# A decoder layer with routed experts on one core: row stores on ACT's queue, the first pair's overflow expert by expert, the last pair by halves of the columns

## The chip, the cores and the metric

One core of a Trainium2 chip. The metric is the time of one execution on the device in microseconds (us); several runs give a median. Times inside an execution are read from one profiled execution and count from the start of its span.

## The reference, cut to what matters

Batch 1, 512 tokens, width 1024, all float32. One layer: attention and a gating MLP side by side, then a mixture of 32 experts in 4 groups of 8.

```python
hn = rmsnorm(h, attn_norm_g); proj = hn @ w_in            # 1024 -> 2560
h = h + concat(rmsnorm(stick_breaking(q, k, v)), rmsnorm(gating(u, vg))) @ w_out
hn = rmsnorm(h, ffn_norm_g)
# one group by argmax, its two best experts; combine = p_group * renormalised p_expert
for g in range(4):                                        # the reference runs all experts
    a = silu(hn @ w_gate[g]) * (hn @ w_up[g])             # 1024 -> 512, per expert
    out = out + (a * combine[:, g]) @ w_down[g]           # 512 -> 1024
return rmsnorm(h + out, final_norm_g)
```

Each expert has 6 MB of weights (2 MB each for gate, up and down); together they are 192 MB that have to be read once. A token goes to two experts, so an expert has some 32 tokens of its own.

## The kernel before, in words

**Stages.** Up to some 215 us the kernel does the projection, attention, gating and the output product. From there on each block of 128 tokens (`c` = 0 to 3) gets its output product (lines 116 to 118, from `u_step`), is added to `h` (DVE, line 621), squared (ACT, 725), transposed (TensorE, 748), sent through the router (`route`, DVE, 757 to 797) and, normalised, stored to DRAM: `with_gain` (POOL, line 737; the last half on DVE) writes `h` times the gain to a tile `xn`, of which there are two, and `store_xn` (739 to 742) scales it on ACT and stores it to `xn_d`. The tile of block 0 is used again for block 2. Behind the router, the list of tokens by expert is built, and POOL gathers rows of `xn_d` by an indirect DMA: 64 slots for each of the two experts of a pair, 128 rows of 4 KB.

**The experts.** 16 pairs (loop from line 1150). For each: `gu(e)` multiplies the gathered rows with the gate and up weights (line 974, two halves of TensorE's columns at once), ACT copies the result (980), `act(e)` transposes and applies the gate (992, 984, 986), `combine` adds the pair before into `h` (TensorE 1028, DVE 1034), `down(p)` makes the down products of both experts (1001), `results(p)` splits them into a high and a low part (ACT 1019, DVE 1020). Up to 32 rows that do not fit into the 64 slots are kept apart; `gate_up_over` and `down_over` work on them under a branch, taken if the expert has such rows (`if_over`: TensorE, ACT and DVE each load a count and jump).

**The order of the loads.** Each weight tile of 1 MB has a slot in a ring; 19 slots exist when the experts begin. SP issues all loads in one list (`order`, line 574): for each pair eight of gate and up, then four of down. `load_next(n)` issues the next `n`, each as soon as the work that read the slot's last content is done. In the loop, `load_next(8)` stands behind both experts' gate and up products and their overflow branch, and `load_next(4)` behind the down products and theirs. Ahead of the loop, SP also issues the four stores of `xn_d` between its loads, and a small store `mark_d` that holds it until the first gather has landed. Each DMA of SP also waits until the DMA eight places ahead of it in its row of semaphores is done.

**The tail.** After the last pair: the one-hot of the overflow rows (1191, 1011), `down` with both halves of the columns in one go (1001), the overflow's own result (1197, 1198), `results`, then eight units (block, half of the columns): three products each (1225, 1028), a sum into `h` (1034) and a sum of squares (ACT, 1204); `scale_3` makes the scale (DVE 1208, POOL 1209), `finish` multiplies with the final gain (DVE 1218, in two cases ACT 1215 and POOL 1216) and stores 256 KB (1219).

Of the kernel before, what the change touches and what calls it, by code (L numbers as in the profile page):

```python
# [19 lines left out]
P = 128  # L20
T = 512
NCH = 4
D = 1024
KD = 8
NH = 8
E = 32
F = 512
# [44 lines left out]
def layer_kernel(ctx, tc, xr, xT, gT, w_inT, w_inR, sgg, wsT, bsp, sbg, sog, w_out, ffp, ffg, wr, br,  # L72
# [501 lines left out]
    order = []  # L574
    for p in range(E // 2):
        order += [(2 * p + r, i, j) for r in range(2) for j in range(2) for i in range(2)]
        order += [(2 * p + r, 2, j) for j in range(2) for r in range(2)]
    slots = []

    def half_slot(pool, tag="b"):  # L580
# [2 lines left out]
    def load_next(n=1):  # L583
        for _ in range(min(n, len(order))):
            e, i, j = order.pop(0)
            slots.append(slots.pop(0))
            t_ = slots[-1](f"r{e}_{i}_{j}")
            dma(t_, (w_gate, w_up, w_down)[i][e][:, j * 2048:(j + 1) * 2048])
            for m in range(2):
                W[e, i, 2 * j + m] = t_[:, m * 1024:(m + 1) * 1024]  # L590
# [356 lines left out]
    XS, GU, SG, HT, YS, OHT = {}, {}, {}, {}, {}, {}  # L947

    def bank(name, *shape):
        return psm.tile([P, *shape], F32, tag="m", name=name)  # L950
# [41 lines left out]
            nc.tensor.transpose(ft[:, j], SG[e][:, j], identf)  # L992
        HT[e] = gated(e, ft, SLOTS, "g")

    def down(p, n_last=False):
        YS[p] = [bank(f"y{p}_{n}", 512) for n in range(2)]
        for j, n in ([(0, 0), (0, 1), (1, 0), (1, 1), (2, 0), (3, 0), (2, 1), (3, 1)] if n_last else
                     [(j, n) for j in range(4) for n in range(2)]):
            for r, rs_ in halves:
                e = 2 * p + r  # L1000
                nc.tensor.matmul(YS[p][n][rs_], HT[e][:, j], W[e, 2, j][:, n * 512:(n + 1) * 512],  # L1001
                                 start=j == 0, stop=j == 3, skip_group_check=True)

    def places(p):
# [9 lines left out]
    def results(p):  # L1014

        yh, yl = (mo.tile([P, D], F32R, tag=t_, name=f"{t_}{p}") for t_ in ("yh", "yl"))
        for n in range(2):
# [4 lines left out]
        YS[p] = (yh, yl)  # L1022

    def add_rows(ps, p, u, first, last):

        c, n = divmod(u, 2)
        for i, y in enumerate(YS[p]):
# [90 lines left out]
    def gate_up_over(p):  # L1118

        for r in range(2):  # L1120
            so[2 * p + r] = xgo[:, r * 512:(r + 1) * 512].rearrange("s (j p) -> s j p", j=4)
        with if_over(66 + p):
            for e in (2 * p, 2 * p + 1):
                with if_over(34 + e):
                    ps = psg.tile([P, F], F32, tag="gu", name=f"go{e}")
                    for kk in range(4):
                        for q, rs_ in enumerate(quads):
                            k, i = 2 * kk + q // 2, q % 2
                            nc.tensor.matmul(ps[rs_], xso[:, k], W[e, i, kk][:, k % 2 * 512:(k % 2 + 1) * 512],
                                             start=kk == 0, stop=kk == 3, skip_group_check=True)  # L1130
                    nc.scalar.activation(so[e], ps.rearrange("s (p j) -> s j p", j=4), AF.Copy,
                                         scale=tabo[:, 2 + e:3 + e])

    def down_over(p):
        with if_over(66 + p):  # L1135
            for e in (2 * p, 2 * p + 1):
                with if_over(34 + e):
                    ft = bank(f"fo{e}", 4, SLOTS)
                    for j in range(4):
                        nc.tensor.matmul(ft[:, j], so[e][:, j], fold, start=j == 0, stop=j == 3,  # L1140
                                         skip_group_check=True)
                    ht = gated(e, ft, OVER, "o")
                    for jj in range(2):
                        for q, rs_ in enumerate(quads):
                            j, n = 2 * jj + q % 2, q // 2
                            nc.tensor.matmul(yo[rs_], ht[:, j], W[e, 2, j][:, n * 512:(n + 1) * 512], start=False,
                                             stop=False, skip_group_check=True)


    for p in range(NP):  # L1150
        a, b = 2 * p, 2 * p + 1
        gu(a)
        if p == 0:
            prep(xso, xgo, "o")
            clear(True)
            pst = bank("pst", 2, NP)
            for i in range(8):
                for r, rs_ in halves:
                    nc.tensor.matmul(pst[rs_], ohf[:, i], cf[:, i, :, r::2], start=i == 0, stop=i == 7,
                                     skip_group_check=True)  # L1160
# [32 lines left out]
    down(p, True)  # L1193
    yo2 = mo.tile([P, 2, 512], F32R, tag="xs", name="yo2")
    YO = [yo2[:, n] for n in range(2)]
    for n, rs_ in halves:
        nc.scalar.activation(YO[n][:SLOTS], yo[rs_], AF.Copy, scale=tabo[rs_, 1:2])
        nc.vector.scalar_tensor_tensor(YO[n][SLOTS:], yo[rs_], tabo[rs_, 1:2], YO[n][:SLOTS].bitcast(F32),
                                       op0=OP.mult, op1=OP.subtract)
    results(p)  # L1200
    ms3 = mo.tile([P, NCH, 2], F32, name="ms3")
    rs3 = mo.tile([P, NCH], F32, name="rs3")
    def squares(c, n):
        nc.scalar.activation(sq, h[:, c, n * 512:(n + 1) * 512], AF.Square, scale=1.0 / 32.0,  # L1204
                             accum_out=ms3[:, c, n:n + 1])
# [5 lines left out]
    def finish(c, n, shared=False):  # L1211
        cs = slice(n * 512, (n + 1) * 512)
        to, src, sc = fin[c][:, cs], h[:, c, cs], rs3[:, c:c + 1]
        if shared:
            nc.scalar.activation(to, src, AF.Copy, scale=sc)  # L1215
            nc.gpsimd.tensor_tensor(to, to, finB[:, cs], op=OP.mult)
        else:
            nc.vector.scalar_tensor_tensor(to, src, sc, finB[:, cs], op0=OP.mult, op1=OP.mult)  # L1218
        dma(out[c * P:(c + 1) * P, cs], to)

    sq = mo.tile([P, 512], F32, tag="sg", bufs=2, name="sq")

    def unit(c, n):
        ps = bank(f"cl{c}_{n}", 512)
        nc.tensor.matmul(ps, oho[:, c * P:(c + 1) * P], YO[n], start=True, stop=False, skip_group_check=True)
        add_rows(ps, p, 2 * c + n, False, True)
        into_h(ps, 2 * c + n)
        squares(c, n)
# [80 lines left out]
    with tc.If(n_over > OVER):  # L1309
# [20 lines left out]
            squares(c, 1)  # L1330
            scale_3(c)
        for c in range(NCH):
            for n in range(2):
                finish(c, n)
    begin.close()


# [52 lines left out]
```

## Time and profile before

| | us |
|---|---|
| median of 3 runs | 768.15 (763.91 to 768.45) |
| the profiled execution | 767.29 |
| its span | 765.5 |
| TensorE busy | 707.2 (92%) |
| DVE busy | 307.5 (40%) |
| ACT busy | 215.1 (28%) |
| POOL busy | 95.6 (12%) |
| moved by DMA | 231.59 MB, mean 303 GB/s |

The busy time of an engine is the union of its instructions; an engine that is busy need not be the one that the others wait for. Rows of a timeline give start, duration, engine, line, operation, result and operands, a count where equal rows are merged, and in square brackets the idle time ahead and what ended it. `PEq`, `SPq` and the like are an engine's sequencer.

### The profile page before, as it was taken

How to read it: one execution, taken by the hardware profiler on the slowest of the kernel's cores; microseconds unless marked ns; L12 is line 12 of the kernel's file. 1: busy time of each engine (PE TensorE's matmuls, PEld its weight loads, DVE VectorE, ACT ScalarE, POOL GpSimd, SP SyncE). 2: the span in 40 equal slices, each digit the busy share in tenths (PEclk: the TensorE clock that was granted, in tenths of full speed). 3: DMA queues.
4: the chain of work that ended last, by engine and by line, in shares of the span. 5: the costliest groups of instructions: out<-in, count | busy, mean ns of one | idle time of the engine just before them, and what ended most of it. 6: DMA issues, size and time to landing. Idle time of an engine off the chain costs nothing. (4 is left out here: it accounts for less than half of the span.)

```text
span 765.5 us, 9186 instructions
## 1 busy us (share of the span) xinstructions
PE 707.2 (92%) x3426; PEld 400.1 (52%) x3426; DVE 307.5 (40%) x538; ACT 215.1 (28%) x328; POOL 95.6 (12%) x88
## 2 busy tenths in 40 slices
PE   9999999999999699999999988999999999898991
PEld 7776666778787544443443434344344444244350
DVE  5556848455764811322431404033043133043065
ACT  6565755655433301111111111111111111111123
POOL 1322212115243310000000000000000000000003
PEclk9999979899999599999999999999999999999996
DMA  8711000217359339999999999999999999999933
GB/s 294 311 45 67 25 30 28 83 52 304 125 218 417 132 131 371 418 420 418 419 420 420 417 422 418 421 419 421 418 419 417 421 419 419 419 419 420 417 132 115
DMA packets 41435, 231.59 MB, mean 303 GB/s; under 512 B 6290, under 2 KB 7954, under 8 KB 16786
## 3 DMA queue, kind: packets, MB, share of 16 engines
q1 hardware_dynamic: 39010, 226.43, 72.8%
q0 software_dynamic: 2352, 4.20, 1.5%
q8 instruction: 44, 0.72, 0.4%
q14 instruction: 29, 0.24, 0.1%
HBM read 230.74 MB, written 4.19 MB: 307 GB/s over the span
## 5 line engine op out<-in xcount | busy, mean ns | idle before, releaser
L974 PE MATMUL gu<-r,xs 128*64 128x512 f32 x1024 | 230.5, 596 | 12.8 <-DMA r<-w_up 8.1
L974 PEld LDWEIGHTS gu<-r,xs 128*64 128x64 f32 x1024 | 84.4, 137 | 158.2 <-issue 134.1
L1001 PE MATMUL y<-r,hg 128*64 128x512 f32 x512 | 114.1, 595 | 3.3 <-ACTq L1135 2.9
L986 DVE TENSOR_TENSOR hg<-ft,gg 128x256 f32<-128x256 f32 x32 | 13.4, 420 | 247.0 <-ACT gg L984 247.0
L980 ACT COPY sg<-gu 128x512 f32<-128x512 f32 x32 | 18.7, 586 | 228.9 <-PE gu L974 228.9
L1034 DVE TENSOR_TENSOR h<-cb,h 128x512 f32<-128x512 f32 x120 | 74.2, 681 | 0.0
L1001 PEld LDWEIGHTS y<-r,hg 128*64 128x64 f32 x512 | 37.2, 137 | 69.9 <-issue 58.6
L914 POOL DMA_INDIRECT xg<-xn_d,gi x16 | 16.2, 1010 | 395.8 <-PE px L960 388.7
L1020 DVE SCALAR_TENSOR_TENSOR yl<-y,tab,yh 128x512 fp32r<-128x512 f32 x32 | 23.8, 750 | 71.2 <-ACT yh L1019 69.8
L1028 PE MATMUL cb<-yh,oh 128*128 128x512 f32 x120 | 49.9, 416 | 0.0
L1028 PE MATMUL cb<-yl,oh 128*128 128x512 f32 x120 | 47.4, 395 | 0.0
L1019 ACT ACTIVATE yh<-y,tab 128x512 fp32r<-128x512 f32 x32 | 21.8, 687 | 87.0 <-PE y L1001 86.1
L116 PE MATMUL pT<-xhi,hl_w 128*128 128x512 f32 x80 | 34.4, 430 | 0.0
L118 PE MATMUL pT<-xhi,hl_w 128*128 128x512 f32 x80 | 33.0, 413 | 0.0
L117 PE MATMUL pT<-xlo,hl_w 128*128 128x512 f32 x80 | 33.0, 413 | 0.0
L111 POOL TENSOR_TENSOR hl_w<-wqk,hl_w 128x1024 fp32r<-128x1024 f32 x10 | 24.3, 2433 | 66.1 <-ACT hl_w L110 63.7
L116 PE MATMUL pR<-hl_w,xhi 128*128 128x512 f32 x64 | 26.1, 408 | 0.0
L117 PE MATMUL pR<-hl_w,xhi 128*128 128x512 f32 x64 | 25.6, 400 | 0.0
L118 PE MATMUL pR<-hl_w,xlo 128*128 128x512 f32 x64 | 25.5, 398 | 0.0
L992 PEld LDWEIGHTS ft<-identf,sg 128*128 128x128 f32 x128 | 14.6, 140 | 20.4 <-issue 18.4
L1028 PEld LDWEIGHTS cb<-yh,oh 128*128 128x128 f32 x120 | 22.6, 188 | 4.5 <-DVE h L1034 0.2
L1028 PEld LDWEIGHTS cb<-yl,oh 128*128 128x128 f32 x120 | 22.7, 189 | 3.7
(263 smaller groups left out, 940.3 us busy)
## 6 DMA issues: line engine op xcount, KB each, us to landing
r<-w_gate SPq DMA_DIRECT2D x64, 1024.0 KB, 20.5
r<-w_up SPq DMA_DIRECT2D x64, 1024.0 KB, 20.0
r<-w_down SPq DMA_DIRECT2D x64, 1024.0 KB, 20.0
wqk<-w_inT SPq DMA_DIRECT2D x10, 512.0 KB, 5.5
wr<-w_inR SPq DMA_DIRECT2D x8, 512.0 KB, 6.9
wo<-w_out SPq DMA_DIRECT2D x8, 512.0 KB, 4.6
xt<-xT SPq DMA_DIRECT2D x8, 256.0 KB, 4.5
h<-xr SPq DMA_DIRECT2D x4, 512.0 KB, 9.9
```

The lines of the kernel that those rows point to most:

```text
L111: (nc.gpsimd if pool else nc.vector).tensor_tensor(lo, src, hi.bitcast(F32), op=OP.subtract)
L116: nc.tensor.matmul(ps, lh, rh, start=first, stop=False)
L117: nc.tensor.matmul(ps, lh, rl, start=False, stop=False)
L118: nc.tensor.matmul(ps, ll, rh, start=False, stop=last)
L914: nc.gpsimd.indirect_dma_start(out=to, out_offset=None, in_=xn_d, in_offset=bass.IndirectOffsetOnAxis(ap=idx, axis=0), bounds_check=T - 1, ...
L974: nc.tensor.matmul(ps[rs_], xs[:, k], w, start=k == 0, stop=k == KD - 1, skip_group_check=True)
L980: nc.scalar.copy(SG[e], GU[e].rearrange("s (p j) -> s j p", j=4))
L1001: nc.tensor.matmul(YS[p][n][rs_], HT[e][:, j], W[e, 2, j][:, n * 512:(n + 1) * 512], start=j == 0, stop=j == 3, skip_group_check=True)
L1019: nc.scalar.activation(yh[:, cs], YS[p][n], AF.Copy, scale=tab[:, 1, p:p + 1])
L1020: nc.vector.scalar_tensor_tensor(yl[:, cs], YS[p][n], tab[:, 1, p:p + 1], yh[:, cs].bitcast(F32), op0=OP.mult, op1=OP.subtract)
L1028: nc.tensor.matmul(ps, OHT[p][:, c * P:(c + 1) * P], y[:, n * 512:(n + 1) * 512], start=first and i == 0, stop=last and i == 1, skip_group ...
L1034: nc.vector.tensor_tensor(h[:, c, cs], ps, h[:, c, cs], op=OP.add)
```

## The change

Four edits, in the order of the program.

1. `store_xn` issues its store from ACT's queue instead of SP's.
2. In the first pair, `gate_up_over` is called for each expert behind its own gate and up products, with `load_next(4)` behind each, and the branch on the pair's count around it is left out. The other pairs do as before.
3. The last pair's down weights are loaded by halves of the columns (4 pieces of 512 columns for each partition, 2 KB each) instead of by halves of the rows.
4. The tail goes by halves: down products, result and four units of the first half, then the same of the second. DVE multiplies the first half of `h` with the gain early (`gained`), ACT scales it when the scale is there, DVE does the second half; POOL has no product in it any more.

```diff
-        order += [(2 * p + r, 2, j) for j in range(2) for r in range(2)]
+        order += [(2 * p + r, 2 + (p == E // 2 - 1), j) for j in range(2) for r in range(2)]
...
+            if i == 3:
+                W[e, i, j] = t_.rearrange("p (j c) -> p j c", j=4)
+                dma(W[e, i, j], w_down[e].rearrange("p (j c) -> p j c", j=4)[:, :, j * 512:(j + 1) * 512])
+                continue
...
         nc.scalar.activation(xn[c], xn[c], AF.Copy, scale=rs2[:, c:c + 1])
-        dma(xn_d[c * P:(c + 1) * P], xn[c])
+        nc.scalar.dma_start(xn_d[c * P:(c + 1) * P], xn[c])
...
+        if p == 0:
+            gate_up_over(a)
+            load_next(4)
         gu(b)
-        gate_up_over(p)
-        load_next(8)
+        if p == 0:
+            gate_up_over(b)
+            load_next(4)
+        else:
+            with if_over(66 + p):
+                gate_up_over(a)
+                gate_up_over(b)
+            load_next(8)
...
-    for c in range(NCH):
-        unit(c, 0)
-    unit(0, 1)
-    unit(1, 1)
-    scale_3(0)
-    unit(2, 1)
-    scale_3(1)
-    finish(0, 0)
-    unit(3, 1)
-    scale_3(2)
-    finish(0, 1)
+    down(p, (0,))
+    results(p, (0,))
+    for c in range(NCH):
+        unit(c, 0)
+        squares(c, 0)
+    down(p, (1,))
+    for c in range(NCH):
+        gained(c)
+    results(p, (1,))
+    for c in range(NCH):
+        unit(c, 1)
+        squares(c, 1)
+        if c:
+            scale_3(c - 1)
+        if c > 1:
+            finish(c - 2)
     scale_3(3)
-    finish(1, 1, True)
-    finish(1, 0)
-    finish(2, 0)
-    finish(2, 1)
-    finish(3, 1, True)
-    finish(3, 0)
+    finish(2)
+    finish(3)
```

SP's queue ahead of the experts, before and then changed; `r` is a weight tile, `xn_d` the stored rows, `mark_d` the small store that waits for the first gather.

```order
L588 DMA r_0_0_1607<-w_gate 128x2048
L588 DMA r_1_0_1609<-w_up 128x2048
L742 DMA xn_d<-xn_1673 128x1024
L742 DMA xn_d<-xn_1739 128x1024
L588 DMA r_0_1_1941<-w_gate 128x2048
L588 DMA r_1_1_1943<-w_up 128x2048
L742 DMA xn_d<-xn_1824 128x1024
L588 DMA r_0_0_1994<-w_gate 128x2048
L742 DMA xn_d<-xn_1924 128x1024
L919 DMA mark_d<-xg 1x16
```

```order
L592 DMA r_0_0_1607<-w_gate 128x2048
L592 DMA r_1_0_1609<-w_up 128x2048
L592 DMA r_0_1_1941<-w_gate 128x2048
L592 DMA r_1_1_1943<-w_up 128x2048
L592 DMA r_0_0_1994<-w_gate 128x2048
L923 DMA mark_d<-xg 1x16
```

The four stores have left SP's queue; the loads and `mark_d` keep their order. They stand in ACT's queue now, each behind its own scaling (here the first and the second; `sqj` is the square of a half block, `hT` the copy of a transposed one):

```order
L745 ACTIVATE xn_1673<-xn_1673,rs_1620 128x1024
L746 DMA xn_d<-xn_1673 128x1024
L729 ACTIVATE sqj,msh<-h 128x512
L754 COPY hT_1_1780<-pt_1_1775 128x512
L729 ACTIVATE sqj,msh<-h 128x512
L754 COPY hT_0_1822<-pt_0_1817 128x512
L745 ACTIVATE xn_1739<-xn_1739,rs_1620 128x1024
L746 DMA xn_d<-xn_1739 128x1024
```

So a square and a copy of the next blocks stand behind a store's issue.

TensorE between the products of the first and the second expert, before and then changed; `pxo` are transposes of the overflow rows, `pst` a table of slots, `gu` gate and up products, `go` those of the overflow rows, `cnt` the counts.

```order
L960 MATMUL pxo_2216<-identf,xgo 128x128 x4
L960 MATMUL pxo_2222<-identf,xgo 128x128 x4
L1105 LDWEIGHTS zb
L1105 MATMUL yo<-zb 128x512
L1159 MATMUL pst<-cft,ohf 64x32 x16
L974 MATMUL gu_2251<-r_0_0_1427,xs_2173 64x512
L974 MATMUL gu_2251<-r_1_0_1429,xs_2173 64x512
```

```order
L964 MATMUL pxo_2216<-identf,xgo 128x128 x4
L964 MATMUL pxo_2222<-identf,xgo 128x128 x4
L1112 LDWEIGHTS zb
L1112 MATMUL yo<-zb 128x512
L1162 MATMUL pst<-cft,ohf 64x32 x16
L1120 TENSOR_LOAD cnt
L1120 ISA x2
L1128 COMPARE_AND_BRANCH
L1133 MATMUL go_2264<-r_0_0_1208,xso 32x512
```

The first branch, with its load of the count, now stands ahead of the second expert's products.

DVE in the tail, before and then changed; `yl` is the low part of a half's down result, `cl` a unit's product, `fin` the output tile, `ms` a sum of squares, `rs` a scale.

```order
L1020 SCALAR_TENSOR_TENSOR yl_6794<-y_0_6770,tab,yh_6793 128x512
L1020 SCALAR_TENSOR_TENSOR yl_6794<-y_1_6771,tab,yh_6793 128x512
L1034 TENSOR_TENSOR h<-cl_0_6802,h 128x512
L1034 TENSOR_TENSOR h<-cl_0_6808,h 128x512
L1034 TENSOR_TENSOR h<-cl_0_6814,h 128x512
L1034 TENSOR_TENSOR h<-cl_0_6820,h 128x512
L1034 TENSOR_TENSOR h<-cl_1_6826,h 128x512
```

```order
L1028 SCALAR_TENSOR_TENSOR yl_6788<-y_0_6777,tab,yh_6787 128x512
L1041 TENSOR_TENSOR h<-cl_0_6791,h 128x512
L1041 TENSOR_TENSOR h<-cl_0_6797,h 128x512
L1041 TENSOR_TENSOR h<-cl_0_6803,h 128x512
L1041 TENSOR_TENSOR h<-cl_0_6809,h 128x512
L1230 TENSOR_TENSOR fin_6697<-h,fin_6699 128x512 x2
L1230 TENSOR_TENSOR fin_6698<-h,fin_6699 128x512 x2
L1028 SCALAR_TENSOR_TENSOR yl_6788<-y_1_6778,tab,yh_6787 128x512
L1041 TENSOR_TENSOR h<-cl_1_6831,h 128x512
```

The second half's low part has moved behind the four sums of the first half and four products with the gain.

## Rows read from the trace of the kernel before

**Rows 1.** The page's slices, 40 of 19.1 us each: GB/s moved.

```profile
GB/s 294 311 45 67 25 30 28 83 52 304 125 218 417 132 131 371 418 420 418 419 420 420 417 422 418 421 419 421 418 419 417 421 419 419 419 419 420 417 132 115
```

**Rows 2.** Timeline of SP's queue, 215 to 300 us.

```profile
230.26 8.54 SPq L742 DMA_DIRECT2D xn_d<-xn  x2
...
268.48 0.33 SPq L588 DMA_DIRECT2D r<-w_gate  x1
287.58 0.33 SPq L588 DMA_DIRECT2D r<-w_up  x1
```

**Rows 3.** DMA issues (count, KB each, us to landing): 255 to 275, 287.6, 290.0 us.

```profile
xn_d<-xn SPq DMA_DIRECT2D x1, 512.0 KB, 3.1
xg<-xn_d,gi POOLq DMA_INDIRECT x2, 4.5
...
r<-w_up SPq DMA_DIRECT2D x1, 1024.0 KB, 5.0
...
xg<-xn_d,gi POOLq DMA_INDIRECT x1, 9.6
```

**Rows 4.** Timelines of POOL, DVE and TensorE, 225 to 292 us.

```profile
245.15 1.60 POOL L737 TENSOR_TENSOR xn<-h,ffB 128x512 f32<-128x512 f32 x1 [9.90 <-DMA xn_d<-xn]
...
240.40 0.24 DVE L787 TENSOR_SCALAR oab<-o_s,o_m 128x32 bf16<-128x32 f32 x1
...
242.40 0.75 DVE L621 SCALAR_TENSOR_TENSOR h<-o,rb,h 128x512 f32<-128x512 f32 x1 [1.64 <-PE o L118]
248.30 0.26 DVE L770 SCALAR_TENSOR_TENSOR L<-lg,rs,brB 128x36 f32<-128x36 f32 x1 [5.15 <-POOL rs L177]
...
252.89 0.74 DVE L621 SCALAR_TENSOR_TENSOR h<-o,rb,h 128x512 f32<-128x512 f32 x1
...
246.52 0.39 PE L118 MATMUL o<-hl_o,m 128*128 128x512 f32 x1
...
253.69 1.11 PE L748 MATMUL pt<-identf,h 128*128 128x128 f32 x4 [3.94 <-DVE h L621]
```

**Rows 5.** TensorE, 268 to 340 us: timeline; then lines 1113 and 1122, 278 to 292.

```profile
271.17 7.09 PE L974 MATMUL gu<-r,xs 128*64 128x512 f32 x32 [0.24 <-ACT xs L961]
...
280.38 7.07 PE L974 MATMUL gu<-r,xs 128*64 128x512 f32 x32
287.76 1.06 PE L992 MATMUL ft<-identf,sg 128*128 128x128 f32 x8 [0.31 <-PEq L1122]
...
297.68 13.95 PE L974 MATMUL gu<-r,xs 128*64 128x512 f32 x64 [0.30 <-PEq L1135]
...
325.23 13.95 PE L974 MATMUL gu<-r,xs 128*64 128x512 f32 x64 [0.31 <-PEq L1135]
...
L1113 PEldq TENSOR_LOAD <-cnt x1: 486/486/486, 283.1 to 283.1; - x1
...
L1122 PEldq COMPARE_BRANCH x1: 367/367/367, 284.0 to 284.0; - x1
```

**Rows 6.** The tail: timelines, 715 to 766 us; last, a window (busy times, PEclk, DMA).

```profile
726.39 3.65 PE L974 MATMUL gu<-r,xs 128*64 128x512 f32 x14 [1.30 <-DMA r<-w_up]
...
735.82 7.09 PE L1001 MATMUL y<-r,hg 128*64 128x512 f32 x32
...
740.71 0.76 DVE L1198 SCALAR_TENSOR_TENSOR yo<-yo,tabo,yo 64x512 fp32r<-64x512 f32 x1 [0.75 <-ACT yo L1197]
...
742.83 0.50 PE L1225 MATMUL cl<-yo,oho 128*128 128x512 f32 x1
...
748.25 0.40 PE L1028 MATMUL cl<-yl,oh 128*128 128x512 f32 x1
...
750.79 7.17 SPq L1219 DMA_DIRECT2D res<-fin  x8
...
752.34 4.74 DVE L1218 SCALAR_TENSOR_TENSOR fin<-h,rs,fin 128x512 f32<-128x512 f32 x4
...
476.00:478.00 2.00, 2.00 (x12) 0.41 (x6) 0.00 (x0) 0.00 (x0) 0.00 (x0) 0.50 1.01 422
```

More of the change, by code (lines that the diff above doesn't have):

```diff
@@ L946, in layer_kernel @@
     NP = E // 2
-    XS, GU, SG, HT, YS, OHT = {}, {}, {}, {}, {}, {}
+    XS, GU, SG, HT, YS, YT, OHT = {}, {}, {}, {}, {}, {}, {}
     def bank(name, *shape):
@@ L993, in act, with down_weights, down @@
         HT[e] = gated(e, ft, SLOTS, "g")
[L995 to L998, printed above, removed]
+    def down_weights(e, j, n):
+        return W[e, 3, n][:, j] if (e, 3, n) in W else W[e, 2, j][:, n * 512:(n + 1) * 512]
+    def down(p, ns=(0, 1)):
+        YS.setdefault(p, [bank(f"y{p}_{n}", 512) for n in range(2)])
+        for j, n in [(j, n) for j in range(4) for n in ns]:
             for r, rs_ in halves:
                 e = 2 * p + r
-                nc.tensor.matmul(YS[p][n][rs_], HT[e][:, j], W[e, 2, j][:, n * 512:(n + 1) * 512],
+                nc.tensor.matmul(YS[p][n][rs_], HT[e][:, j], down_weights(e, j, n),
                                  start=j == 0, stop=j == 3, skip_group_check=True)
@@ L1012, in tokens, with results @@
                                 at[:, :, None].to_broadcast([P, NCH, P]), op=OP.is_equal)
-    def results(p):
-        yh, yl = (mo.tile([P, D], F32R, tag=t_, name=f"{t_}{p}") for t_ in ("yh", "yl"))
-        for n in range(2):
+    def results(p, ns=(0, 1)):
+        if p not in YT:
+            YT[p] = [mo.tile([P, D], F32R, tag=t_, name=f"{t_}{p}") for t_ in ("yh", "yl")]
+        yh, yl = YT[p]
+        for n in ns:
             cs = slice(n * 512, (n + 1) * 512)
@@ L1021, in results @@
                                            op0=OP.mult, op1=OP.subtract)
-        YS[p] = (yh, yl)
     def add_rows(ps, p, u, first, last):
         c, n = divmod(u, 2)
-        for i, y in enumerate(YS[p]):
+        for i, y in enumerate(YT[p]):
             nc.tensor.matmul(ps, OHT[p][:, c * P:(c + 1) * P], y[:, n * 512:(n + 1) * 512], start=first and i == 0,
@@ L1116, in if_over, with gate_up_over @@
         return tc.If(n > 0)
[L1118 to L1132, printed above, removed]
+    def gate_up_over(e):
+        so[e] = xgo[:, e % 2 * 512:(e % 2 + 1) * 512].rearrange("s (j p) -> s j p", j=4)
+        with if_over(34 + e):
+            ps = psg.tile([P, F], F32, tag="gu", name=f"go{e}")
+            for kk in range(4):
+                for q, rs_ in enumerate(quads):
+                    k, i = 2 * kk + q // 2, q % 2
+                    nc.tensor.matmul(ps[rs_], xso[:, k], W[e, i, kk][:, k % 2 * 512:(k % 2 + 1) * 512],
+                                     start=kk == 0, stop=kk == 3, skip_group_check=True)
+            nc.scalar.activation(so[e], ps.rearrange("s (p j) -> s j p", j=4), AF.Copy, scale=tabo[:, 2 + e:3 + e])
     def down_over(p):
@@ L1145, in down_over @@
                             j, n = 2 * jj + q % 2, q // 2
-                            nc.tensor.matmul(yo[rs_], ht[:, j], W[e, 2, j][:, n * 512:(n + 1) * 512], start=False,
+                            nc.tensor.matmul(yo[rs_], ht[:, j], down_weights(e, j, n), start=False,
                                              stop=False, skip_group_check=True)
@@ L1192, in layer_kernel @@
     tokens(oho, tabot)
-    down(p, True)
     yo2 = mo.tile([P, 2, 512], F32R, tag="xs", name="yo2")
-    YO = [yo2[:, n] for n in range(2)]
     for n, rs_ in halves:
-        nc.scalar.activation(YO[n][:SLOTS], yo[rs_], AF.Copy, scale=tabo[rs_, 1:2])
-        nc.vector.scalar_tensor_tensor(YO[n][SLOTS:], yo[rs_], tabo[rs_, 1:2], YO[n][:SLOTS].bitcast(F32),
+        nc.scalar.activation(yo2[:SLOTS, n], yo[rs_], AF.Copy, scale=tabo[rs_, 1:2])
+        nc.vector.scalar_tensor_tensor(yo2[SLOTS:, n], yo[rs_], tabo[rs_, 1:2], yo2[:SLOTS, n].bitcast(F32),
                                        op0=OP.mult, op1=OP.subtract)
-    results(p)
     ms3 = mo.tile([P, NCH, 2], F32, name="ms3")
     rs3 = mo.tile([P, NCH], F32, name="rs3")
+    sq = mo.tile([P, 512], F32, tag="sg", bufs=2, name="sq")
     def squares(c, n):
@@ L1209, in scale_3, with gained, finish @@
         nc.gpsimd.tensor_tensor(rs3[:, c:c + 1], ms3[:, c, :1], mhalf[:, :1], op=OP.pow)
[L1211 to L1221, printed above, removed]
     def unit(c, n):
         ps = bank(f"cl{c}_{n}", 512)
-        nc.tensor.matmul(ps, oho[:, c * P:(c + 1) * P], YO[n], start=True, stop=False, skip_group_check=True)
+        nc.tensor.matmul(ps, oho[:, c * P:(c + 1) * P], yo2[:, n], start=True, stop=False, skip_group_check=True)
         add_rows(ps, p, 2 * c + n, False, True)
         into_h(ps, 2 * c + n)
-        squares(c, n)
+    def gained(c):
+        nc.vector.tensor_tensor(fin[c][:, :512], h[:, c, :512], finB[:, :512], op=OP.mult)
+    def finish(c):
+        sc = rs3[:, c:c + 1]
+        nc.scalar.activation(fin[c][:, :512], fin[c][:, :512], AF.Copy, scale=sc)
+        nc.vector.scalar_tensor_tensor(fin[c][:, 512:], h[:, c, 512:], sc, finB[:, 512:], op0=OP.mult, op1=OP.mult)
+        for n in range(2):
+            cs = slice(n * 512, (n + 1) * 512)
+            dma(out[c * P:(c + 1) * P, cs], fin[c][:, cs])
+    down(p, (0,))
+    results(p, (0,))
     for c in range(NCH):
         unit(c, 0)
-    unit(0, 1)
-    unit(1, 1)
-    scale_3(0)
-    unit(2, 1)
-    scale_3(1)
-    finish(0, 0)
-    unit(3, 1)
-    scale_3(2)
-    finish(0, 1)
-    scale_3(3)
-    finish(1, 1, True)
-    finish(1, 0)
-    finish(2, 0)
-    finish(2, 1)
-    finish(3, 1, True)
-    finish(3, 0)
+        squares(c, 0)
[10 more added lines that the diff above has]
+            finish(c - 2)
+    scale_3(3)
+    finish(2)
+    finish(3)
     EN = [ET.PE, ET.Activation, ET.DVE, ET.Pool, ET.SP]
@@ L1332, in layer_kernel @@
         for c in range(NCH):
-            for n in range(2):
-                finish(c, n)
+            gained(c)
+            finish(c)
     begin.close()
```

## Prediction

> **What bounds the kernel now.** I read the slices of the page first, then SP's timeline, and then the engines around the places where SP waits.
>
> The slices [rows 1] show two stages. In the first fifteen, up to 287 us, the transfers come in bursts, and slices 14 and 15 (248.8 to 287.1 us) move 132 and 131 GB/s. From slice 17 to slice 37 every slice moves some 420 GB/s, without a gap. A load of 1 MB (1.0486 million bytes) takes 1.0486 / 0.419 = 2.50 us there. A pair of experts needs 12 loads and a gather of 0.5 MB: 12 x 2.50 + 1.25 = 31.25 us. TensorE needs 325.23 - 297.68 = 27.55 us for a pair [rows 5]. So the second stage is bound by the transfers, TensorE has 3.7 us to spare in each pair, and what counts is how early the stream begins and how long the tail behind it is.
>
> The stream begins late. SP [rows 2] issues load 19 at 268.48 and load 20 only at 287.58. All 19 slots hold a load then, load 20 needs the first slot of expert 0, and SP gets it when TensorE has finished the gate and up products of both experts of the first pair and the branch behind them: TensorE's next work stands at 287.76 [rows 5]. Nineteen microseconds without an issue are worth little more than five of transfers (what was in flight still lands), so the DMA engines are nearly idle for some 13 us. Any microsecond by which load 20 comes earlier is one at the end, as long as TensorE follows.
>
> The stage ahead of it waits for a transfer too. POOL's product for the third block of tokens starts at 245.15 after 9.90 us of waiting for the store of the first block [rows 4]. That store was issued at 230.26 [rows 2] on SP, behind the weight loads that stood in SP's queue by then. DVE's logits of the third block wait for POOL until 248.30, TensorE, which had its products done at 246.52 + 0.39 = 246.91, waits 3.94 us for DVE's last sum, which starts at 252.89 [rows 4]. From there over the first gather to the first product at 271.17 [rows 5] is a chain of small instructions without any gap of note.
>
> The tail is bound by TensorE, DVE and ACT. The last products wait for the last up weights until 726.39, the down products run from 735.82 to 742.91 without a wait for weights [rows 6].
>
> **The stores (A).** Four stores go from SP's queue to ACT's, 512 KB each. What does the first one take there? Alone, such a store lands after 3.1 us [rows 3]. For a second queue beside SP's full one the nearest row is the gather, of the same size: 4.5 us on idle engines, 9.6 with SP's loads ahead of it [rows 3], so 5.1 us more. From both sides, the store lands between 230.3 + 3.1 = 233.4 and the 245.1 of now; I take 230.3 + 3.1 + 5.1 = 238.5, since that row is a transfer of this size on another queue beside the same loads. POOL's product then ends at 240.1, its small instructions behind it wait for DVE's mask (240.40 + 0.24 [rows 4]) and end near 242.1. DVE can start the third block's logits behind its sum at 242.40 + 0.75 = 243.15, in place of 248.30: 5.15 us earlier. TensorE's own limit for the last sum is 246.95 in place of 252.89: 5.9 us. I take 5.4. On ACT each store costs an issue, 0.33 us as on SP [rows 2], between activations that wait for others anyway; the one ahead of the last square is in the 0.5 us by which I stay below 5.9. Stores two to four land long before the gather asks for them; SP, rid of its wait for ACT, can issue load 17 some microseconds earlier, which fills idle engines. Bounds of A: 0 and 6.5.
>
> The Trainium skill speaks against this part: "DMA: Bandwidth & Descriptors", section "Issuing engines are not separate DMA queues", says that DMAs started by different engines run on the same 16 DMA engines and interleave, so that a second issuing engine saves only the time of issuing. By that A would be some 0.3 us. The row of the gather agrees with the interleaving, and what I expect comes from just that: interleaved, the store isn't behind SP's loads any more. It is rival 1.
>
> **Expert 0 by itself (B).** In the first pair the branch for slots over 64 comes behind each expert's products, and four loads behind each. TensorE starts the second expert's products at 280.38 [rows 5]; there the first branch stands now. From the start of its load of the count, 283.1, to the end of the jump, 284.0 + 0.37, it was 1.25 us [rows 5]. Before, this ran in TensorE's sequencer while products were still running, and cost 0.31 [rows 5]; now only the short transposes stand ahead of it, so I count all of it, 1.2 us. Load 20 is released at 281.6 instead of 287.58: 6.0 earlier. Below, the whole is hidden (7.2 earlier); above, the branch waits for DVE and ACT as well, another 1 us (5 earlier). The second branch costs what the old one did. Neither expert takes the branch: nothing of line 1129 stands in that stretch.
>
> Does the lead survive? With A and B, load 20 is issued at 287.58 - 11.4 = 276.2 and lands 5.0 later [rows 3], 281.2. Loads 21 to 31 follow at 2.50, with a gather: load 31 at 281.2 + 27.5 + 1.25 = 309.9. Load 32 needs the slots of the second pair's gate and up weights. These products ended at 297.68 + 13.95 = 311.63 [rows 5]; they move by -5.4 + 1.2 to 307.4. Load 32 should be issued by 309.9 + 2.5 - 5.0 = 307.4. It is just in time, and later pairs gain 3.7 us each. So the lead of 11.4 holds, with nothing to spare: each microsecond that TensorE is later costs nearly one.
>
> **The tail (C).** The last pair's four down loads come by halves of the columns, in rows of 2 KB instead of 8. They are needed 9 and 18 us after the last up weights; four loads at 2.50 are 10 us, and even half as much again hides. TensorE does the first half's products (7.09 / 2 = 3.55 us, from 735.82), then needs the first half's result. That hangs on ACT and DVE, which are at the overflow rows until 740.71 + 0.76 = 741.47 [rows 6]; the result's low part ends at 742.2, so TensorE idles from 739.4 to about 742. Four units of 0.69 (eight take from 742.83 to 748.65 [rows 6], the end of the last included) bring it to 745.0, the second half's products to 748.5, another result of 1.5 to 750.0, the last units to 752.5. Before it was done at 748.65. Against this, what follows the last unit is shorter: half of the squares and adds are done, POOL's product of 1.5 us beside DVE, under which DVE's four last products took 4.74 / 4 = 1.2 us each and not the 0.76 of the one at 740.71 [rows 6], goes, and ACT takes one half. I get the last products at 757.1 and the last issue near 758.0; before, the issues ended at 750.79 + 7.17 = 757.96 [rows 6]. So nothing; I add 0.5 for the risk in the gaps. Bounds: -1.5 and +3.4 (rival 2).
>
> **Sum.** The profiled execution took 767.29 us, 765.5 of them its span; the median of the runs is 768.15. 767.3 - 5.4 - 6.0 + 0.5 = 756.4 us.
>
> **Rivals.**
> 1. The store lands no earlier on ACT's queue, as transfers share the engines. For it: slice 13, up to 248.8 us, moves 417 GB/s [rows 1], so the engines are full. Against it: the gather's 9.6 us beside queued loads. A is nothing, the time 767.3 - 6.0 + 0.5 = 761.8.
> 2. TensorE's clock falls in the tail. In the window 476 to 478 it was granted 0.50 [rows 6], 1.2 of 2.4 GHz, in the middle of the second stage, where TensorE does the small products of the overflow branch and waits for DVE between them. The new gap of 2.6 us is alike. Against it: TensorE is busy ahead of the gap and has the first unit's two other products in it. If the fall covers the four units and a little more, 3.4 us of work takes 6.8: 767.3 - 11.4 + 3.4 = 759.3.
> 3. The change doesn't do what it says: SP's loads are released no earlier than before, because the slot's release is bound to something behind the second expert's products. For it: SP's wait names the branch, not the product. Against it: only the first expert's products read these slots. B becomes the cost of the branch: 767.3 - 5.4 + 0.5 = 762.4.
> 4. Slower: the engines serve SP's queue first while it holds loads. SP no longer waits for the stores, so loads 15 to 17 would go ahead of the first two stores, and these land near 255. POOL then starts at 255 instead of 245.15, the chain to the gather is 9.9 us later: 767.3 + 9.9 - 6.0 + 0.5 = 771.7. It decides from a landing at 251 on, where A has eaten B. Against it: the gather's row. The same page of the Trainium skill, section "Queues, rings and completion order", has each engine take turns between its queues, which would exclude this rival; the gather's 9.6 us agree.
>
> **Chances and range.** Forecast 0.60 (752.5 to 760), rival 1 0.15, rival 2 0.15, rival 3 0.05, rival 4 0.05. A change of 1% is about what a measurement of this kernel can tell: 760.5 and 775.8 are the marks. The forecast is nearly all below 760.5 (0.58), so is most of rival 2 (0.11) and a little of 1 and 3 (0.04): faster 0.73. Rival 4 is slower by half a per cent; only its far end and what I have not seen pass 1%: 0.03. The rest, 0.24, is the same. The range reaches from all of A and B with a better tail (767.3 - 6.5 - 7.2 - 1.5 = 752.1, less a little for the spread of the runs) to rivals 1 and 3 with the worse tail: 751.5 to 764.5.
>
> **What would show it.** A: POOL's wait before its third block's product goes from 9.9 to about 3 us and the first product starts near 265.8. B: load 20 at about 276, six or so us after the first expert's products would allow without the branch being more than 1.5 us; slices 14 and 15 move more. No gap in the stream near 307. C: TensorE idle 2 to 3 us between the down halves, the time from the last up weights' landing to the end unchanged within 1 us. It is wrong if the first product still starts at 271 (rivals 1 and 4), if SP still has no issue between 269 and 282 (rival 3), if the stream stops near 307, or if the clock in the tail is below full (rival 2).

## The result and the profile after

The changed kernel takes 754.54 us (median of 4 runs, 754.08 to 755.52); before took 767.13 over four runs beside it. The ratio is 0.9844, interval 0.9809 to 0.9878. The forecast was 756.4 us in a range of 751.5 to 764.5, and a gain of over 1% with a chance of 0.73. The profiled execution took 755.52 us, 753.7 of them its span, so 11.8 us less than the profiled execution of before.

First the start of the stream. The page's GB/s, which answers to [rows 1] (slices of 18.8 us now):

```profile
GB/s 307 307 35 78 6 50 29 84 61 299 129 203 424 197 262 419 400 419 420 417 422 419 417 422 418 421 418 416 423 419 417 421 417 419 420 418 420 396 104 117
```

Slices 14 and 15 (245 to 283 us) move 197 and 262 GB/s and from slice 16 on the stream is full; before that was so from slice 17 on. SP's timeline, against [rows 2]: load 19, load 20, load 32.

```profile
260.62 0.33 SPq L592 DMA_DIRECT2D r<-w_gate  x1
273.12 0.33 SPq L592 DMA_DIRECT2D r<-w_up  x1
...
304.57 0.33 SPq L592 DMA_DIRECT2D r<-w_up  x1
```

Timelines of ACT, POOL, DVE and TensorE, against [rows 4, 5]:

```profile
227.45 0.35 ACTq L746 DMA_DIRECT2D xn_d<-xn  x1
...
235.84 1.65 POOL L741 TENSOR_TENSOR xn<-h,ffB 128x512 f32<-128x512 f32 x1 [3.40 <-DMA xn_d<-xn]
...
246.30 0.66 PE L752 MATMUL pt<-identf,h 128*128 128x128 f32 x4 [1.38 <-DVE h L625]
...
263.10 7.09 PE L978 MATMUL gu<-r,xs 128*64 128x512 f32 x32 [0.24 <-ACT xs L965]
...
271.36 1.12 PE L1162 MATMUL pst<-cft,ohf 128*64 128x32 f32 x32
273.15 7.09 PE L978 MATMUL gu<-r,xs 128*64 128x512 f32 x32 [0.67 <-PEq L1128]
```

POOL waits 3.40 us where it waited 9.90, and TensorE 1.38 where it waited 3.94. The branch holds TensorE for 0.67 us ahead of the second expert, and load 20 goes out at that moment.

Not all of this is the change. The sum into `h` of the first block is ahead of everything that was touched, and it came 2.81 us earlier. DVE's row of before, and then of after:

```profile
218.56 0.75 DVE L621 SCALAR_TENSOR_TENSOR h<-o,rb,h 128x512 f32<-128x512 f32 x1 [1.23 <-PE o L118]
```

```profile
215.75 0.75 DVE L625 SCALAR_TENSOR_TENSOR h<-o,rb,h 128x512 f32<-128x512 f32 x1 [1.23 <-PE o L118]
```

So I cut every profile at four marks that all of them have: H, the start of this sum; G, the first gate and up product; S, the issue of load 20; U, the last 14 gate and up products, which wait for the last up weights; and the end of the span. In us; before ran beside each of them (medians 767.13 to 769.02), and the ratio is to those runs; "old", "split" and "filled" say which tail a kernel has:

| kernel | median of runs | ratio to before, interval | H | G - H | S - G | U - G | end - U | tail |
|---|---|---|---|---|---|---|---|---|
| before | 767.13 | | 218.56 | 52.61 | 16.41 | 455.22 | 39.11 | old |
| changed | 754.54 | 0.9844, 0.9809 to 0.9878 | 215.75 | 47.35 | 10.02 | 449.90 | 40.70 | split |
| a_only | 759.32 | 0.9898, 0.9863 to 0.9933 | 221.24 | 47.80 | 16.41 | 454.82 | 38.64 | old |
| b_only | 761.97 | 0.9930, 0.9903 to 0.9956 | 214.68 | 54.70 | 11.22 | 450.31 | 39.01 | old |
| ab | 754.30 | 0.9843, 0.9801 to 0.9886 | 216.26 | 47.45 | 10.02 | 449.59 | 38.10 | old |
| c_only | 769.66 | 1.0041, 1.0014 to 1.0068 | 215.84 | 53.30 | 16.41 | 455.07 | 42.09 | split |
| d_tail | 756.12 | 0.9832, 0.9804 to 0.9859 | 220.42 | 47.33 | 10.06 | 449.35 | 37.70 | filled |
| rows_8k | 757.93 | 0.9852, 0.9814 to 0.9890 | 219.19 | 46.59 | 10.75 | 450.99 | 41.03 | split |
| no_branch | 754.74 | 0.9842, 0.9810 to 0.9873 | 215.93 | 46.24 | 3.68 | 448.33 | 41.70 | split |
| all_again | 758.28 | 0.9854, 0.9823 to 0.9885 | 220.60 | 47.23 | 10.02 | 450.39 | 40.08 | split |
| two_pairs | 752.96 | 0.9806, 0.9762 to 0.9851 | 217.35 | 47.75 | 10.03 | 449.36 | 37.44 | filled |
| late_pst | 752.63 | 0.9803, 0.9761 to 0.9846 | 219.27 | 46.98 | 8.78 | 448.28 | 37.57 | filled |

For the changed kernel the 11.8 us are 2.8 of H, 5.3 of G - H, 5.3 of U - G, and 1.6 given back behind U. Where they were given back, TensorE, DVE and SP in the tail, against [rows 6]:

```profile
713.00 3.65 PE L978 MATMUL gu<-r,xs 128*64 128x512 f32 x14 [1.28 <-DMA r<-w_up]
...
722.48 3.65 PE L1007 MATMUL y<-r,hg 128*64 128x512 f32 x16
...
727.80 0.50 PE L1035 MATMUL cl<-yh,oh 128*128 128x512 f32 x1 [0.93 <-ACT yh L1027]
...
731.17 3.65 PE L1007 MATMUL y<-r,hg 128*64 128x512 f32 x16
...
736.40 0.50 PE L1035 MATMUL cl<-yl,oh 128*128 128x512 f32 x1 [0.29 <-DVE yl L1028]
...
738.59 0.40 PE L1035 MATMUL cl<-yl,oh 128*128 128x512 f32 x1
...
741.96 1.41 DVE L1235 SCALAR_TENSOR_TENSOR fin<-h,rs,fin 128x512 f32<-128x512 f32 x2 [0.16 <-POOL rs L1220]
...
740.75 5.83 SPq L1238 DMA_DIRECT2D res<-fin  x8
```

TensorE waits for ACT and DVE in front of each half's units and ends at 738.99, 26.0 us behind U; before it was 748.65 - 726.39 = 22.3. The first store goes out 27.75 us behind U (before 24.40). DVE is done at 743.37, but SP needs until 746.58 to issue the eight stores, 3.2 us longer; before it was done 0.9 us behind DVE (757.96 against 757.08).

### The profile page after: what moved, and what is told of

Same layout as the page of the kernel before. It is cut to its first block, busy times and chain, and to the rows that moved or that the text cites. A ratio compares the mean times of both kernels' runs of the same rounds, so it can differ in the third digit from the quotient of the medians.

```text
span 753.7 us, 9185 instructions
## 1 busy us (share of the span) xinstructions
PE 700.1 (93%) x3426; PEld 395.0 (52%) x3426; DVE 308.0 (41%) x540; ACT 216.1 (29%) x330; POOL 92.1 (12%) x86
## 5 line engine op out<-in xcount | busy, mean ns | idle before, releaser
L978 PE MATMUL gu<-r,xs 128*64 128x512 f32 x1024 | 228.1, 594 | 10.9 <-DMA r<-w_up 5.3
L990 DVE TENSOR_TENSOR hg<-ft,gg 128x256 f32<-128x256 f32 x32 | 13.4, 420 | 242.0 <-ACT gg L988 242.0
L984 ACT COPY sg<-gu 128x512 f32<-128x512 f32 x32 | 18.8, 586 | 223.8 <-PE gu L978 223.8
L116 PE MATMUL pT<-xhi,hl_w 128*128 128x512 f32 x80 | 33.6, 420 | 0.0
L996 PEld LDWEIGHTS ft<-identf,sg 128*128 128x128 f32 x128 | 14.6, 140 | 20.5 <-issue 18.3
```

The source lines that it names most:

```text
L116: nc.tensor.matmul(ps, lh, rh, start=first, stop=False)
L978: nc.tensor.matmul(ps[rs_], xs[:, k], w, start=k == 0, stop=k == KD - 1, skip_group_check=True)
L984: nc.scalar.copy(SG[e], GU[e].rearrange("s (p j) -> s j p", j=4))
```

## The experiments

**Each part alone.** The stores alone on the kernel before:

```diff
-        dma(xn_d[c * P:(c + 1) * P], xn[c])
+        nc.scalar.dma_start(xn_d[c * P:(c + 1) * P], xn[c])
```

> The kernel before with the stores of the normalised rows alone moved to ACT's queue. Theory (each part works by itself and they add): the first store lands 8.2 us after its issue as in the changed kernel, POOL waits 3.4 us in place of 9.9, the first product starts 5.3 us earlier against the first block's sum into h, the rest of the stream keeps its shape: 5.3 us faster than before. Rival 1 (the stores save only an issue): under 1 us. Rival N (needs the second part to be worth anything): under 2 us. Whatever the head up to the first block's sum takes (218.56 us before, 215.75 in the changed kernel, no instruction of it was touched) is chance, so compare from there.

Ratio 0.9898. The DMA issue (to landing 8.4 us), POOL and TensorE:

```profile
xn_d<-xn ACTq DMA_DIRECT2D x1, 512.0 KB, 8.4
```

```profile
241.46 1.62 POOL L737 TENSOR_TENSOR xn<-h,ffB 128x512 f32<-128x512 f32 x1 [3.53 <-DMA xn_d<-xn]
...
269.04 7.09 PE L974 MATMUL gu<-r,xs 128*64 128x512 f32 x32 [0.24 <-ACT xs L961]
```

G - H falls by 4.8 us to 47.80, U - G stays. The store lands 8.4 us after its issue, and POOL is let go 8.5 us after it (232.9 to 241.46). On SP's queue, where the profile has no landing time for this store, POOL was let go 14.89 us after the issue (230.26 to 245.15). The issue itself stands 11.7 us behind H in both. So the gain is the landing, not the issue, and rival 1 is out. From H to the end the profile is 5.7 us shorter; the runs say 7.8, interval 5.1 to 10.5.

The branches alone, the stores on SP (`gate_up_over` takes one expert, as in the change; the other pairs keep both calls and `load_next(8)`):

```diff
+        if p == 0:
+            gate_up_over(a)
+            load_next(4)
         gu(b)
-        gate_up_over(p)
-        load_next(8)
+        if p == 0:
+            gate_up_over(b)
+            load_next(4)
...
```

> The kernel before with the first pair's overflow branches alone set expert by expert. Theory: POOL still waits 9.9 us, load 20 is issued some 6 us earlier against the start of the first product (10.0 us behind it in place of 16.4), and the stream keeps 5 of these, since load 32 is then just in time: 5 to 6 us faster. Rival (the stream stops again at load 32 and gives most back): under 2 us.

Ratio 0.9930, so 5.4 us by the runs. In the profile S - G is 11.22, not 10.0, and G - H is 2.1 us longer than before, which nothing in the edit does. TensorE, and then the window 262 to 272 (columns as in [rows 6], the clock third from the end):

```profile
264.19 3.50 PE L1084 MATMUL pso<-ovr,ohv 128*128 128x34 f32 x16
...
269.38 8.29 PE L974 MATMUL gu<-r,xs 128*64 128x512 f32 x32
```

```profile
262.00:272.00 10.00, 10.00 (x50) 7.83 (x50) 3.63 (x11) 0.59 (x1) 2.58 (x4) 0.51 0.64 231
```

TensorE was granted half its clock (0.51, the level of 1.2 GHz) up to the middle of the first products. These took 8.29 us and not 7.09; `pso` took 3.50, where it took 1.94 in before, and the transposes behind it 1.95, where they took 1.07. Cut at G, the part is worth 455.22 - 450.31 = 4.9 us. In rows_8k and late_pst too the clock was still low when the first products began (they took 7.79 and 7.64 us), so S - G there holds some of it.

Both of these diffs together (ab), and on the kernel before the last pair's loads and tail of the change alone (c_only):

```diff
-        order += [(2 * p + r, 2, j) for j in range(2) for r in range(2)]
+        order += [(2 * p + r, 2 + (p == E // 2 - 1), j) for j in range(2) for r in range(2)]
...
-    down(p, True)
...
+    down(p, (0,))
+    results(p, (0,))
...
```

> Stores on ACT's queue and the branches expert by expert, the last pair as in the kernel before. Theory: the tail by halves costs 1.6 to 2.0 us (in the profiles 33.6 us from the last up weights to the last store's issue in place of 31.6), so this is 1 to 2 us faster than the changed kernel: a ratio to before near 0.983 and a time of 753. Rival (the tail by halves is worth something): 1 us slower than the changed kernel or more, 756.

> The kernel before with the last pair's down weights and the tail by halves alone. Theory: 1 to 2 us slower than before, ratio 1.001 to 1.003, the stream ahead of it unchanged. Rival (the tail by halves gains, and the rest of the measured 12.6 us is its): 2 to 3 us faster, ratio 0.997.

A and B come to 0.9843 and a profile whose G - H and U - G are those of the changed kernel within 0.4 us: the parts add. By the runs, 7.8 and 5.4 us apart make 13.2, and ab has 12.1 (interval 8.8 to 15.3). Its ratio can't be told from that of the changed kernel (0.9844 and 0.9854), so what the split tail costs is read from c_only and from end - U. The last pair alone is slower, 1.0041 with an interval clear of 1 (1.1 to 5.2 us). By end - U the split tail takes 40.70, 40.08 and 41.03 us in three profiles, the old one 38.10 to 39.11 in four: some 2 us. In c_only it took 42.09, since there the clock fell. The window between its halves:

```profile
737.00:740.00 3.00, 1.30 (x4) 0.37 (x2) 2.18 (x4) 1.37 (x2) 0.00 (x0) 1.00 0.00 0
740.00:744.00 4.00, 3.87 (x10) 2.94 (x10) 2.09 (x4) 1.44 (x4) 0.00 (x0) 0.57 0.00 0
```

TensorE was busy for 1.30 of 3.00 us in front of the first units, and while it did them the clock was 0.57; a product took 0.63 us in place of 0.40. That is rival 2. It shows in two of the five profiles with the split tail (c_only, and no_branch with 0.51 from 727 to 730.5 us), TensorE's end then 27.8 and 27.5 us behind U in place of 26.0, and in none of the seven with another tail. What decides it is open: in front of the first units TensorE was busy for 1.48 of 3.00 us in the changed kernel (726 to 729) and kept its clock, and for 1.72 of 3.00 in no_branch (724 to 727) and lost it. The Trainium skill, "TensorE: Matmul & The Clock Gate", Part 1, section "What's actually happening", says of the start of a kernel that the number of products at the low clock differs from run to run of one kernel. No run here shows that of a tail; the two profiles of the changed kernel both kept their clock there.

**The tail's loads.** The changed kernel with the old loads:

```diff
-        order += [(2 * p + r, 2 + (p == E // 2 - 1), j) for j in range(2) for r in range(2)]
+        order += [(2 * p + r, 2, j) for j in range(2) for r in range(2)]
```

> The changed kernel with the last pair's down weights loaded by halves of the rows (8 KB pieces), the tail by halves kept. Theory (2 KB pieces cost the load nothing that is waited for): the last down load lands 9.9 us after the last up load as in the kernel before, the first half's products may wait 1 us for it, and the time is within 1 us of the changed kernel. Rival (the 2 KB pieces slow the loads and are what the tail loses): 2 us faster.

757.93 us beside 758.28 of the changed kernel in the same set. The last load landed 9.9 us behind the last up load, with 2 KB pieces 10.6 to 10.7: 0.7 us for which nothing waits. The pieces aren't what the tail loses.

**A tail without the gap.** Both halves' down products ahead of the first unit, the gain's products between the last sums:

```diff
     down(p, (0,))
     results(p, (0,))
+    down(p, (1,))
+    results(p, (1,))
     for c in range(NCH):
         unit(c, 0)
         squares(c, 0)
-    down(p, (1,))
-    for c in range(NCH):
-        gained(c)
-    results(p, (1,))
     for c in range(NCH):
         unit(c, 1)
         squares(c, 1)
         if c:
+            gained(c - 1)
             scale_3(c - 1)
         if c > 1:
             finish(c - 2)
+    gained(3)
     scale_3(3)
```

> The changed kernel with the down products of both halves one behind the other ahead of the first unit, the gain's products on DVE put between the sums of the second half. Theory (the tail by halves loses because TensorE has nothing to do between the halves, 2.5 us in front of the first units and 1.1 in front of the second, and because all eight stores of 256 KB then come out together, SP issuing them one behind the other until 3.2 us after the last product): TensorE ends 22.5 us after the start of its last gate and up piece in place of 26.0, the first store is issued some 2.5 us earlier, DVE ends about where it did, and the last store lands 3 us earlier: 2 to 4 us faster than the changed kernel, 0.5 to 1.5 faster than the kernel with the old tail. Rival (the tail is set by DVE's sum of work): within 1 us of the changed kernel.

TensorE, DVE and SP, with U at 717.10:

```profile
726.52 7.09 PE L1007 MATMUL y<-r,hg 128*64 128x512 f32 x32
...
738.96 0.40 PE L1035 MATMUL cl<-yl,oh 128*128 128x512 f32 x1
...
744.76 1.42 DVE L1235 SCALAR_TENSOR_TENSOR fin<-h,rs,fin 128x512 f32<-128x512 f32 x2 [0.32 <-POOL rs L1220]
...
741.80 5.49 SPq L1238 DMA_DIRECT2D res<-fin  x8
```

TensorE ends 22.3 us behind U, the first store goes out at 24.7 (3.05 us sooner than in the changed kernel), SP is done at 30.2 where it was 33.6, and 1.1 us behind DVE where it was 3.2. End - U is 37.70, 3.0 us below the changed kernel and 0.4 to 1.4 below the old tails. DVE's end moved only from 30.4 to 29.1 us behind U, so the rival's bound is near. The time was set by the gaps and by how late the stores came out, as the theory had it; the order of the products and the place of the gain's products moved together, and no run parts them. By the runs alone (756.12 beside 758.28) the intervals overlap.

**How far the lead carries.** The first pair without its branches; it leaves out the products of the rows over 64 of experts 0 and 1 (these two have none: the first such product in the changed kernel starts at 443.3 us).

```diff
-            gate_up_over(a)
+            no_over(a)
             load_next(4)
...
-            gate_up_over(b)
+            no_over(b)
```

> The changed kernel without the two branches of the first pair; it leaves out the products of the rows over 64 of experts 0 and 1. Theory (the branch costs TensorE 0.7 to 0.9 us ahead of the second expert, and load 20 waits for it, but the stream loses most of this at load 32): the second expert's products start 9.2 us behind the first's in place of 10.05, load 20 is issued up to 2.8 us earlier, and the stream from load 33 on is 1 to 1.5 us earlier. Rival (the lead is capped elsewhere): the stream from load 33 on is unchanged.

Load 20 and load 32 on SP:

```profile
265.85 0.33 SPq L592 DMA_DIRECT2D r<-w_up  x1
...
302.50 0.33 SPq L592 DMA_DIRECT2D r<-w_up  x1
```

Load 20 goes out 3.68 us behind G, 6.3 earlier than in the changed kernel, more than either theory had: without a branch a slot is free as soon as the half of the products that reads it is done. How far ahead of before a load landed, both times counted from H, in us:

| load | changed | no_branch | d_tail | two_pairs | late_pst |
|---|---|---|---|---|---|
| 20 | 11.8 | 17.7 | 11.6 | 11.3 | 13.4 |
| 29 | 11.8 | 17.2 | 11.5 | 11.2 | 13.3 |
| 35 | 10.5 | 13.0 | 11.4 | 11.2 | 13.9 |
| 188 | 10.6 | 13.3 | 11.2 | 10.7 | 12.6 |

Without the branches the lead holds to load 29 and drops by 4.2 us by load 35. Load 32, issued at 302.50, needs the second pair's products, and load 31 had landed at 301.96: the engines had run dry. U - G ends only 1.6 us below the changed kernel. The lead ends there as forecast, at TensorE's pace.

**Moving that limit.** On the kernel with the filled tail, the second pair expert by expert too:

```diff
-        if p == 0:
+        if p < 2:
             gate_up_over(a)
             load_next(4)
...
-        if p == 0:
+        if p < 2:
             gate_up_over(b)
```

> The kernel with the filled tail (both halves' down products ahead of the units), and the overflow branches expert by expert in the second pair too, so that load 32 waits for the third expert's products and not for both of the second pair. Theory (load 32 is where the lead is cut, by 0.8 to 1.3 us): the stream loses nothing there, the last gate and up piece starts 495.4 to 496.0 us behind the first block's sum in place of 496.7, the run is about 1 us faster. Rival (the cut lies elsewhere, and the new branch ahead of the fourth expert's products costs TensorE 0.8 us that the stream pays at load 44): 497 to 497.5.

and with that the small products ahead of the first branch (`clear` and `pst`) moved behind the second expert's:

```diff
             prep(xso, xgo, "o")
-            clear(True)
-            pst = bank("pst", 2, NP)
...
         gu(b)
+        if p == 0:
+            clear(True)
+            pst = bank("pst", 2, NP)
...
```

> As the kernel with two pairs expert by expert, and the 33 small products between the first expert's and the branch (the clearing of the overflow sums and the table of slots, 1.4 us) moved behind the second expert's products. Theory (load 20 waits for all that stands ahead of the branch): load 20 is issued 8.6 us behind the first product in place of 10.05, and with load 32 no longer cutting the lead some 1 us of this is left at the end: 494.5 to 495.5 us from the first block's sum to the last gate and up piece. Rival (TensorE's pace sets the stream in the first pairs, so an earlier load 20 is worth nothing): as the kernel with two pairs, within 0.4 us.

Load 32 in two_pairs, then load 20 in late_pst (its G is 266.25):

```profile
299.63 0.33 SPq L592 DMA_DIRECT2D r<-w_up  x1
```

```profile
275.03 0.33 SPq L592 DMA_DIRECT2D r<-w_up  x1
```

In two_pairs load 32 goes out 6.5 us sooner against H than in d_tail (82.28 for 88.76), and U - G is the same (449.36 for 449.35). My theory was wrong there: in d_tail load 32 landed 2.5 us behind load 31, so nothing was lost that could come back. The loss at load 32 was 1.3 us in the changed kernel and 1.6 in all_again, 0.45 in ab. With the limit moved, an earlier load 20 seems to carry: in late_pst it goes out 8.78 us behind G and U - G is 1.1 us lower, as forecast. It is one profile, and the kernels with the branches set expert by expert spread over 1.6 us in U - G (449.35 to 450.99); no run has the later products without the second pair's branches; and the runs, 752.96 and 752.63, can't tell these two apart. Both are below before by 1.9% and 2.0%, against 1.5 to 1.6% for the changed kernel.

**Chance in the head.** The changed kernel again:

> The changed kernel once more, beside the others on one chip, since the head up to the first block's sum took 2.8 us less in its profile than in that of before, with fewer microseconds at the half clock, and no instruction there is touched. Theory (the head's time is chance): 10 us faster than before over many runs, ratio 0.987, with single runs spread over 4 us or more. Rival (the change also speeds the head): ratio 0.984 and below, with a narrow spread.

Ratio 0.9854, runs from 754.16 to 761.10, H at 220.60. Windows 0 to 200 us of b_only, before, and a_only, H 214.68, 218.56 and 221.24:

```profile
0.00:200.00 200.00, 190.92 (x876) 143.24 (x877) 119.90 (x142) 118.30 (x145) 49.26 (x39) 0.97 0.36 129
```

```profile
0.00:200.00 200.00, 192.77 (x848) 144.71 (x849) 117.36 (x139) 117.14 (x143) 49.42 (x38) 0.95 0.35 125
```

```profile
0.00:200.00 200.00, 193.06 (x826) 144.36 (x827) 115.72 (x137) 115.71 (x141) 48.28 (x37) 0.92 0.35 125
```

The granted clock of the head is 0.97, 0.95 and 0.92. All twelve profiles order alike: 0.97 goes with H at 214.7 to 215.9, 0.96 with 216.3 to 217.4, 0.95 with 218.6, 0.94 with 219.2 and 219.3, 0.93 with 220.4 and 220.6, 0.92 with 221.2. The two profiles of the changed kernel stand near both ends of it (0.97 and 0.93), so H is not the change's. The narrow spread of the first four runs, 1.4 us, did not come again: here it is 6.9.

## Why the prediction was right

**What bounds it.** Right. What load 20 gained came out at the end, but for about one microsecond.

**A.** Right in size and in mechanism. Forecast: the store lands 3.1 + 5.1 = 8.2 us after its issue. Measured: 8.4 in a_only, and POOL is let go at 235.84 in the changed kernel, 8.4 behind the issue. The first product was to come 5.4 us earlier, and comes 5.3 earlier against H. The row of the gather beside loads was the right one to read. The Trainium skill's rule ("DMA: Bandwidth & Descriptors", section "Issuing engines are not separate DMA queues"), that a second issuing engine saves only the time of issuing, does not hold here: POOL is let go 6.5 us sooner after the store's issue (8.39 for 14.89), and the issue takes 0.33. That the transfers interleave, which the same section says, fits this: on a queue of its own the store takes more than the 3.1 us of idle engines, but no longer stands behind SP's loads.

Part of the size is luck all the same. The last sum into `h`, for which the 5.4 were worked out, comes 4.57 us earlier against H (29.76 behind it for 34.33); the other 0.7 lie behind it, where the last block's products for the router ran faster. The sum in the changed kernel, then these products in before and in the changed kernel:

```profile
245.51 0.74 DVE L625 SCALAR_TENSOR_TENSOR h<-o,rb,h 128x512 f32<-128x512 f32 x1
```

```profile
255.53 1.92 PE L754 MATMUL lg<-wrs,hT 128*128 128x36 f32 x8 [0.57 <-ACT hT L750]
```

```profile
247.63 1.08 PE L758 MATMUL lg<-wrs,hT 128*128 128x36 f32 x8 [0.50 <-ACT hT L754]
```

TensorE's granted clock was 0.50 from 250 to 255 us before, behind its wait of 3.94 us, and 0.91 from 245 to 250 us in the changed kernel. In a_only the sum is 4.57 earlier too, but these products took 1.92 us, and G - H fell by 4.8. In rows_8k, no_branch and late_pst the sum comes 5.9 us earlier, which is TensorE's own limit as the working had it.

**B.** Right. The branch was to cost 1.2 us on TensorE; the second expert's products start 10.05 us behind the first's where they started 9.21 behind, so 0.84. Load 20 was to be 6.0 us earlier against G and is 6.39 earlier; at the end U - G is 5.3 lower, so 0.7 of the term is missing there.

**Does the lead survive.** Nearly right: "just in time". The working had load 32 needed 2.5 us ahead of load 31's landing; it was issued 2.7 ahead (304.57 against 307.25), and 1.3 us were lost there. The sum had the lead hold whole; it was 11.8 us at load 20 and 10.6 at load 188. no_branch shows what is behind this: 6 us more of lead are worth 1.6 in its profile.

**C.** This is the term that was mis-sized: forecast +0.5 within -1.5 to +3.4, measured +1.6 in the profile, some 2 over all profiles, and 1.1 to 5.2 by the runs of c_only. The sign it was given, from the last up weights to the end unchanged within 1 us, failed. The step that failed is "the last issue near 758.0". TensorE's end (26.1 us behind U forecast, 26.0 measured) and DVE's (30.7, 30.4) came out as worked, but I had the last issue 0.9 us behind DVE, as before, and it is 3.2. I had not asked how soon the stores can leave: the split tail makes all eight ready later and within less time, and SP issues them one behind the other for 5.8 us. The gap that I priced at nothing was also open to rival 2, which costs 1.5 to 1.8 us where it comes, half of the 3.4 that I had. The window 476 to 478 from which I took it was misread in part: TensorE is busy for all of it, and its waits (1.19 and 0.74 us, of which only the second is for DVE) lie ahead of it, between 471 and 474.2 us.

**The sum.** The terms were to give -10.9 us against the profiled execution: -5.4 - 6.0 + 0.5. The changed profile has -9.0 apart from H: -5.3 - 5.3 + 1.6. The head's 2.8 us, which are chance, brought it to -11.8. The runs say -11.2 (interval -13.6 to -8.8) and -12.0 (-14.6 to -9.4) in two sets, so they lean to the forecast rather than to the profiles; what stands in these two microseconds between is not settled, as an execution without a profile can't be cut at H.

## What to carry to other kernels

A small store on which an engine waits should not stand in the queue that feeds the big loads: look for the wait named after the DMA, and for a transfer of the same size on another queue to price the move. When a load waits for a slot, ask which wait comes next before counting the whole gain. And a split that lets work start earlier is worth something only if the engine in front has other work for the gap; here the same two halves, with both products first, took 3 us less than with the units between.

## What was not expected

- The head, which no edit touched, moved the whole kernel by 6.6 us (H from 214.68 to 221.24) with the granted clock of the first 200 us between 0.97 and 0.92. Twelve profiles with one time each would have ranked these kernels wrongly; cut at marks that all have, kernels with the same part agree within some 2 us in G - H and U - G, where H differs by 6.6.
- The same products ahead of the first experts' (`pso`) took 1.94 us in before and 3.50 in b_only by the clock they met, on the chain that starts the stream.
- One of SP's eight issues in the tail took 1.62 us, where the median of the eight is 0.45; what held it doesn't show. SP's timeline in the changed kernel, from 741.19 us:

```profile
741.19 1.62 SPq L1238 DMA_DIRECT2D res<-fin  x1
```
